# Expert stage of a hybrid decoder trunk: down weights in chunks of four row blocks by half the columns, the stationary side of the down product exchanged for the small experts, gating by two blocks, another final store

## The chip, the cores and the metric

The kernel runs on one core of a Trainium2 chip. The metric is device time in microseconds, the median of three runs. Engines are named as in the profile: PE is the matrix engine (PEld its weight loads), DVE the vector engine, ACT the scalar engine, POOL the GpSimd engine, SP the queue that issues most DMAs.

## What is computed

Two layers: a gated convolution mixer with a dense feed-forward, then an attention mixer with a routed feed-forward. The change touches only the routed one, here in the reference's words (512 tokens, `d` = 1024, hidden width 2048, 8 experts, each token goes to 2 of them):

```python
def swiglu(h, w_gate, w_up, w_down):
    return (jax.nn.silu(h @ w_gate) * (h @ w_up)) @ w_down

def moe_swiglu(h, router, w_gate, w_up, w_down):
    ...
    out = jnp.zeros_like(ht)
    for e in range(N_EXPERTS):
        out = out + gates[:, e:e + 1] * swiglu(ht, w_gate[e], w_up[e], w_down[e])
```

All of it is float32. The kernel reaches that accuracy with three products of split numbers: each float32 weight is split into a high part (`w_hi`, type fp32r) and the rest (`w_lo`, bf16); each activation likewise into `xe` (high part and rest side by side) and `xb` (bf16).

## The kernel before

**Experts and tokens.** Expert 0 comes first, then the other seven in the order of how many tokens they got. Each has room for a fixed number of tokens, its cap: 152, 152, 144, 140, 132, 128, 124, 116. An expert with a cap of at most 128 has its tokens in one part (`nh` is 1: the last three); the others have two halves (`nh` is 2). More tokens than these caps hold are left to a loop at the end (L1349 on), which does not run for these inputs.

**Chunks and steps.** An expert's weights come as 24 chunks of 1 MB, each [128 x 2048] in float32: 16 chunks for the hidden product (eight gate and eight up blocks of 128 x 128 each) and 8 for the down product (sixteen blocks: all hidden rows of one block of 128 output columns). The loop over `e` and `c` (L1275 on) is a sequence of 192 steps, one per chunk, whose code order is the order of every engine. Each step also splits one chunk ahead: ACT makes `w_hi` (L88), DVE makes `w_lo` (L97), and SP issues the load of a later chunk into a ring of raw buffers that is freed by `w_lo`.

**A hidden step** `c < 16` (`hidden_mm`, `row`): PE multiplies 16 blocks of `w_hi` (stationary) with `xe` (moving, 2 x cap columns; L1033), then 16 blocks of `w_lo` with `xb` (cap columns; L1035), into a PSUM tile `gu`. ACT and DVE add the two halves into `p2` (L1047, L1048). A step later ACT takes the SiLU into `sg` (L1053) and POOL multiplies it with the up half (L1054); another step later the result is split into `ae` and `ab` (L1058 ACT, L1059 DVE, L1060 ACT). So every one of the 16 blocks brings one SiLU, one POOL product and three split instructions.

**A down step** `c >= 16` (`down_mm`): the same 16 + 16 products, with `ae` and `ab` as moving side. Its first step keeps the last two hidden blocks for the end, since they are gated last. The result `y` has the output columns on the partitions, so it must be transposed back (`store_mm`, L1080: 4 transposes per 512 columns), scaled by the gate on ACT (`store_ev`, L1084), and added to `out` in memory row by row by an indirect, accumulating DMA that POOL issues (`store`, L1087).

**Side work of an expert.** `select` (L969, POOL): four comparisons that mark the next expert's tokens in `oh`, at steps 4 to 7. `find` (L976, PE, then small DVE operations): turns `oh` into row numbers, after step 8. `gather` (L996, POOL): an indirect DMA that fetches those rows of `hrow` into `xr`. `load_mm` and `load_ev` (L1011, L1018, L1019): transposes `xr` into the next expert's `xe`, at steps 16 to 22. The previous expert's result is transposed and stored in steps 1 to 4 with the stores issued at step 2 and, for two halves, step 13. The last expert has no next one: its transposes and its store follow its own last steps.

Of the kernel before, what the change touches and what calls it, by code (L numbers as in the profile page):

```python
# [11 lines left out]
F32 = mybir.dt.float32  # L12
# [9 lines left out]
P = 128  # L22
# [133 lines left out]
def hybrid_trunk_kernel(ctx, tc, xT_in, pos_in, vecs_in, rope_g, invf_in, ident_in, cst_in, info_in, dslot_in,  # L156
# [801 lines left out]
    class Expert:  # L958
        def __init__(s, block_row, slot, cap):
            s.block_row, s.slot, s.cap = block_row, slot, cap  # L960
            s.nh = 1 if cap <= P else 2
            s.hc = cap // s.nh
            s.p2, s.sg = {}, {}
# [59 lines left out]
        def row(s, ps, hl, n, x2, xb, flip, late=()):  # L1023

            order = [k for k in range(n) if k not in late]
            for kcs in (order, list(late)):
                for part in ((1, 0) if flip else (0, 1)):
                    for i, p in enumerate(ps):
                        for kc in kcs:
                            first = kc == order[0] and part == (1 if flip else 0)  # L1030
                            final = kc == (late or order)[-1] and part == (0 if flip else 1)
                            if part == 0:
                                mm(p[:, 0:2 * s.cap], hl[i][kc][0], x2[:, kc, :, :], start=first, stop=final)  # L1033
                            else:
                                mm(p[:, 0:s.cap], hl[i][kc][1], xb[:, kc, :], start=first, stop=final)  # L1035

        def hidden_mm(s, f, flip):
# [4 lines left out]
            b = s.block_row(2 * NB)  # L1042
            s.row([s.ps[:, 0], s.ps[:, 1]], [b[0:NB], b[NB:]], NB, s.xe, s.xb, flip)

        def hidden_add(s, f):
            p2 = s.p2[f] = ep2.tile([P, 2, CAP], F32, name="p2")[:, :, 0:s.cap]
# [9 lines left out]
        def hidden_split(s, f):  # L1056
            sg = s.sg.pop(f)
            nc.scalar.copy(s.ae[:, f, 0, :], sg)  # L1058
            tt(s.ae[:, f, 1, :], sg, s.ae[:, f, 0, :].bitcast(F32), ALU.subtract)  # L1059
            nc.scalar.copy(s.ab[:, f, :], sg)  # L1060
# [8 lines left out]
        def down_add(s, fo):  # L1069
            p2 = ep2.tile([P, 2, CAP], F32, name="p2")[:, :, 0:s.cap]  # L1070
            nc.scalar.copy(p2, s.ps[:, :, s.cap:2 * s.cap])
            tt(s.y[:, fo - 1:fo + 1, :], s.ps[:, :, 0:s.cap], p2, ALU.add)
# [19 lines left out]

    def static_row(n):
        return [ws.block() for _ in range(n)]
# [49 lines left out]
    ex = [Expert(static_row, e % 2, CAPS[e]) for e in range(NE)]  # L1144
# [128 lines left out]

    last_k = len(chunks) - 1
    for e in range(NE):  # L1275
        x, nxt, prv = ex[e], ex[e + 1] if e + 1 < NE else None, ex[e - 1] if e else None
        for c in range(24):

            out_x, g = (x, 0) if not nxt and c == NF + 5 else (prv, c - 1)
            storing = out_x and 0 <= g < 2 * out_x.nh  # L1280
            loading = nxt and NF <= c < NF + LOADS
            if storing:
                out_x.store_mm(g)
# [263 lines left out]
```

## Time and profile before

| what | value |
|---|---|
| median of three runs | 1452.95 us (1450.19 to 1458.37) |
| the profiled execution's own time | 1453.82 us |
| its span on the profile | 1452.0 us |
| PE, share of the span busy | 96% |
| DVE, ACT, POOL | 69%, 58%, 20% |
| expert stage | from about 790 us to the end |

The span is the time from the first to the last instruction of one profiled execution; the time of that execution is 1.8 us longer. Busy shares are means over very different stages. Two properties of the records must be kept in mind: the end of a matrix instruction is modelled and lies later than the start of its successor, so that the time of one is read from start to start, and short idle times between two of them disappear; and a wait for several semaphores is put down to the one that came last.

### The profile page before, as it was taken

How to read it: one execution, taken by the hardware profiler on the slowest of the kernel's cores; microseconds unless marked ns; L12 is line 12 of the kernel's file. 1: busy time of each engine (PE TensorE's matmuls, PEld its weight loads, DVE VectorE, ACT ScalarE, POOL GpSimd, SP SyncE). 2: the span in 40 equal slices, each digit the busy share in tenths (PEclk: the TensorE clock that was granted, in tenths of full speed). 3: DMA queues.
4: the chain of work that ended last, by engine and by line, in shares of the span. 5: the costliest groups of instructions: out<-in, count | busy, mean ns of one | idle time of the engine just before them, and what ended most of it. 6: DMA issues, size and time to landing. Idle time of an engine off the chain costs nothing.

```text
span 1452.0 us, 25181 instructions
## 1 busy us (share of the span) xinstructions
PE 1395.4 (96%) x10047; PEld 1230.8 (85%) x10048; DVE 1005.5 (69%) x1332; ACT 836.9 (58%) x1416; POOL 292.9 (20%) x268
## 2 busy tenths in 40 slices
PE   9999999999999999999999989999999999998994
PEld 6888888888888887878867989999999999998983
DVE  7745554432444444677778977888879898898993
ACT  6322333221222333776547768778778888888892
POOL 0000000000000000232303513416161534234240
PEclk9999999999999999999999999999999999999997
DMA  6322322232232232101126998889989999999980
GB/s 216 133 87 88 109 95 87 96 108 87 87 116 88 87 103 79 57 32 59 59 113 215 358 329 291 305 327 312 333 308 346 331 329 336 327 352 344 367 313 16
DMA packets 48884, 284.00 MB, mean 196 GB/s; under 512 B 8928, under 2 KB 10720, under 8 KB 16760
## 3 DMA queue, kind: packets, MB, share of 16 engines
q1 hardware_dynamic: 41688, 269.82, 51.7%
q0 software_dynamic: 7072, 12.51, 3.9%
q8 instruction: 81, 1.33, 0.4%
q14 instruction: 43, 0.35, 0.1%
HBM read 270.91 MB, written 11.37 MB: 194 GB/s over the span
## 4 chain that ended last, share of the span: by engine, by line
PE 70%; ACT 8%; POOL 8%; DVE 7%; issue 4%; DMA 2%; POOLq 0%; SPq 0%; ACTq 0%
PE ps L255 13%; PE ps L256 13%; PE ps L257 13%; PE gu L1033 13%; PE gu L1035 6%; ACT w_hi L88 4%; POOL sg L1054 4%; POOL oh L969 2%; DVE w_lo L97 2%; DMA xr<-hrow,ids 1%; PE ps L643 1%; POOL out L1087 1%; ACT p L1047 1%; PE ps L640 1%; ACT ae L1058 1%
## 5 line engine op out<-in xcount | busy, mean ns | idle before, releaser
L97 DVE TENSOR_TENSOR w_lo<-w_raw,w_hi 128x2048 bf16<-128x2048 f32 (+1 forms) x239 | 547.9, 2293 | 53.6 <-ACT w_hi L88 53.4
L88 ACT CAST w_hi<-w_raw 128x2048 fp32r<-128x2048 f32 x239 | 455.9, 1909 | 208.3 <-PE ps L256 157.9
L1033 PE MATMUL gu<-xe,w_hi 128*128 128x304 f32 (+6 forms) x2048 | 294.5, 297 | 0.0
L1033 PEld LDWEIGHTS gu<-xe,w_hi 128*128 128x128 f32 x2048 | 269.3, 192 | 0.1
L255 PE MATMUL ps<-xh,w_hi 128*128 128x512 f32 x592 | 232.7, 393 | 1.4 <-DVE xT L399 0.9
L256 PE MATMUL ps<-xl,w_hi 128*128 128x512 f32 x592 | 231.5, 391 | 0.0
L257 PE MATMUL ps<-xh,w_lo 128*128 128x512 f32 x592 | 231.2, 390 | 0.0
L1054 POOL TENSOR_TENSOR sg<-sg,p 128x152 f32<-128x152 f32 (+6 forms) x128 | 135.8, 1061 | 355.8 <-ACT sg L1053 352.9
L1035 PEld LDWEIGHTS <-w_lo 128*128 128x128 bf16 x3072 | 182.4, 98 | 19.7 <-DVE w_lo L97 8.2
L1033 PE MATMUL gu<-ae,w_hi 128*128 128x304 f32 (+6 forms) x1024 | 150.9, 297 | 6.0 <-DVE ae L1059 6.0
L1035 PE MATMUL gu<-xb,w_lo 128*128 128x152 bf16 (+6 forms) x2048 | 144.6, 224 | 5.2 <-DVE w_lo L97 4.3
L1033 PEld LDWEIGHTS gu<-ae,w_hi 128*128 128x128 f32 x1024 | 134.6, 190 | 8.4 <-DVE ae L1059 8.3
L255 PEld LDWEIGHTS ps<-xh,w_hi 128*128 128x128 f32 x592 | 111.6, 189 | 26.3 <-ACT xh L290 1.5
L256 PEld LDWEIGHTS ps<-xl,w_hi 128*128 128x128 f32 x592 | 111.6, 188 | 24.2 <-DVE xl L291 0.7
L257 PEld LDWEIGHTS ps<-xh,w_lo 128*128 128x128 f32 x592 | 111.6, 189 | 23.1
L248 POOL TENSOR_TENSOR rs<-m,mhalf 128x4 f32<-128x4 f32 x3 | 3.1, 1021 | 590.7 <-DVE m L505 555.8
L256 PE MATMUL ps<-al,w_hi 128*128 128x512 f32 x240 | 94.8, 395 | 0.0
L257 PE MATMUL ps<-ah,w_lo 128*128 128x512 f32 x240 | 94.8, 395 | 0.0
L255 PE MATMUL ps<-ah,w_hi 128*128 128x512 f32 x240 | 94.7, 395 | 0.0
L1048 DVE TENSOR_TENSOR p<-gu,p 128x304 f32<-128x304 f32 (+6 forms) x128 | 55.6, 434 | 27.7 <-ACT p L1047 23.3
L1035 PE MATMUL gu<-ab,w_lo 128*128 128x152 bf16 (+6 forms) x1024 | 73.6, 224 | 0.0
L1059 DVE TENSOR_TENSOR ae<-sg,ae 128x152 fp32r<-128x152 f32 (+6 forms) x128 | 51.8, 405 | 25.5 <-ACT ae L1058 25.5
(322 smaller groups left out, 1778.0 us busy)
## 6 DMA issues: line engine op xcount, KB each, us to landing
w_raw<-w_moe SPq DMA_DIRECT2D x192, 1024.0 KB, 7.3
w_raw<-w_a SPq DMA_DIRECT2D x50, 1024.0 KB, 4.9
w_raw<-w_hp SPq DMA_DIRECT2D x4, 1088.0 KB, 5.7
w_raw<-w_o SPq DMA_DIRECT2D x4, 1024.0 KB, 4.7
xT<-xT_in SPq DMA_DIRECT2D x8, 256.0 KB, 4.6
out<-hs SPq DMA_DIRECT2D x8, 256.0 KB, 3.4
hrow<-xh POOLq DMA_DIRECT2D x2, 1024.0 KB, 5.9
hrow<-xl POOLq DMA_DIRECT2D x2, 1024.0 KB, 26.3
```

Of the source, the lines that this page charges most:

```text
L88: self.nc.scalar.copy(hi[:, :w], self.raw[k][:, :w])
L97: self.nc.vector.tensor_tensor(lo[:, :w], self.raw.pop(k)[:, :w], self.hi[k][:, :w].bitcast(F32), ALU.subtract)
L255: mm(ps, wh, xh[:, kc, :], start=kc == 0, stop=False)
L256: mm(ps, wh, xl[:, kc, :], start=False, stop=False)
L257: mm(ps, wl, xh[:, kc, :], start=False, stop=kc == n - 1)
L640: mm(ps[:, 0:n], s.qT[h][a][:, q_s], s.kT[h][b][:, 0:n], start=i == 0, stop=False)
L969: nc.gpsimd.tensor_scalar(s.oh[:, tb, 0:s.cap], iota[:, 0:s.cap], p[:, tb], None, op0=ALU.is_equal)
L1033: mm(p[:, 0:2 * s.cap], hl[i][kc][0], x2[:, kc, :, :], start=first, stop=final)
L1035: mm(p[:, 0:s.cap], hl[i][kc][1], xb[:, kc, :], start=first, stop=final)
L1048: tt(p2, s.ps[:, :, 0:s.cap], p2, ALU.add)
L1054: nc.gpsimd.tensor_tensor(sg, sg, p2[:, 1], ALU.mult)
L1059: tt(s.ae[:, f, 1, :], sg, s.ae[:, f, 0, :].bitcast(F32), ALU.subtract)
```

## The change

It changes the routed experts only.

1. The host packs the down weights otherwise: a chunk is now four row blocks of 128 hidden rows by 512 of the 1024 columns, and the 8 chunks are 4 for the first half of the columns, then 4 for the second.
2. `down_mm` follows: step `k` uses the hidden blocks `4 kq` to `4 kq + 3` only (`kq = k % 4`), and its PSUM tiles live for four steps. For an expert of two halves the weights remain stationary (two PSUM tiles of two banks for half the columns). For one with at most 128 tokens `ae` and `ab` become the stationary side and the weights the moving side, 512 columns at a time, 8 + 4 products per step; the result has the tokens on the partitions, so there is no transposing back: `down_add` scales by the gate on its way out of PSUM.
3. `hidden_gate` and `hidden_split` work on two blocks at a time, every second step.
4. `select` moves to the down steps: expert `e` marks in its steps 16 to 19 for expert `e + 2` (for expert 1, expert 0 does so in its steps 2 and 3). `find` and `gather` move from step 8 to step 3 (step 6 in expert 0), and in expert 0 the ranking of the experts moves one or two steps forward.
5. A store of an expert with one part is issued in step 0 of its successor.
6. The last expert fetches its rows of `out` in step 14 (`last_base`), adds the scaled product to them on DVE and writes them back with a plain indirect DMA, one for each half of the columns, after steps 19 and 23 (`last_store`).

```diff
-        def hidden_gate(s, f):
-            sg = s.sg[f] = ep2.tile([P, CAP], F32, name="sg")[:, 0:s.cap]
-            p2 = s.p2.pop(f)
-            act(sg, p2[:, 0], AF.Silu)
-            nc.gpsimd.tensor_tensor(sg, sg, p2[:, 1], ALU.mult)
...
-        def down_mm(s, fo, flip):
-            if fo == 0:
-                s.y = late[0].tile([P, NB, CAP], F32, name="y")[:, :, 0:s.cap]
-            if fo % 2 == 0:
-                s.ps = gps.tile([P, 2, T], F32, name="gu", tag="gu")
-            s.row([s.ps[:, fo % 2]], [s.block_row(NF)], NF, s.ae, s.ab, flip, (NF - 2, NF - 1) if fo == 0 else ())
...
+            hi, lo = s.chunk()
+            for w, x, n in ((hi, s.xe, 2 * s.cap), (lo, s.xb, s.cap)):
+                for i in range(2):
+                    for kc in range(NB):
+                        b = (i * NB + kc) * P
+                        mm(s.ps[:, i, 0:n], w[:, b:b + P], x[:, kc], start=w is hi and kc == 0,
+                           stop=w is lo and kc == NB - 1)
...
+        def hidden_gate(s):
+            s.sg = ep2.tile([P, 2, CAP], F32, name="sg")[:, :, 0:s.cap]
+            act(s.sg, s.p2[:, :, 0], AF.Silu)
+            nc.gpsimd.tensor_tensor(s.sg, s.sg, s.p2[:, :, 1], ALU.mult)
+        def hidden_split(s, i):
+            f = slice(2 * i, 2 * i + 2)
+            nc.scalar.copy(s.ae[:, f, 0, :], s.sg)
+            tt(s.ae[:, f, 1, :], s.sg, s.ae[:, f, 0, :].bitcast(F32), ALU.subtract)
+            nc.scalar.copy(s.ab[:, f, :], s.sg)
+        def down_mm(s, k):
+            hi, lo = s.chunk()
+            kq = k % 4
+            if s.nh == 1:
+                if kq == 0:
+                    s.dp = gps.tile([P, 2, T], F32, name="gu", tag="gu")[0:s.cap, 0]
+                for j in range(4):
+                    for part in range(2):
+                        mm(s.dp, s.ae[:, 4 * kq + j, part, :], hi[:, j * T:(j + 1) * T],
+                           start=kq + j + part == 0, stop=False)
+                for j in range(4):
+                    mm(s.dp, s.ab[:, 4 * kq + j, :], lo[:, j * T:(j + 1) * T], start=False, stop=kq + j == 6)
+                return
+            if kq == 0:
+                s.dp = [gps.tile([P, 2, T], F32, name="gu", tag="gu") for _ in range(2)]
+            for qs in ((0, 1), (2, 3)) if kq == 3 else ((0, 1, 2, 3),):
+                for w, x, n in ((hi, s.ae, 2 * s.cap), (lo, s.ab, s.cap)):
+                    for q in qs:
+                        for j in range(4):
...
+    def last_store(q):
...
+        stt(yt, last.dp, last.gate_ap(0), last.base[:, d], op0=ALU.mult, op1=ALU.add)
+        nc.gpsimd.indirect_dma_start(
+            out=out.rearrange("t (q d) -> (t q) d", q=2),
+            out_offset=bass.IndirectOffsetOnAxis(ap=last.row2[:, q:q + 1], axis=0), in_=yt, in_offset=None)
...
-            if prv and c == 2:
+            if prv and c == (2 if prv.nh == 2 else 0):
                 prv.store(0)
...
-            if nxt and 4 <= c < 4 + TB:
-                nxt.select(posn[:, :, e + 1 - NS:e + 2 - NS], (c - 4,))
-            if nxt and c == 8:
+            if e + 2 < NE and NF <= c < NF + TB:
+                ex[e + 2].select(posn[:, :, e + 2 - NS:e + 3 - NS], (c - NF,))
+            if nxt and c == (3 if e else 6):
                 nxt.find(e + 1)
                 nxt.gather()
```

**On POOL's queue**, from the store of expert 5's result on, in expert 6 (`sg` is the product of the gating, `oh` the marks for expert 7, `xr` the gather of its rows). Before:

```order
L1087 DMA out<-yt_13398,ids_11470 664x1024
L1054 TENSOR_TENSOR sg_13541<-sg_13541,p2_13494 128x124
L1054 TENSOR_TENSOR sg_13589<-sg_13589,p2_13544 128x124
L969 TENSOR_SCALAR oh_13601<-rest_109,posn_6113 128x116
L1054 TENSOR_TENSOR sg_13639<-sg_13639,p2_13592 128x124
```

The next rows are three more pairs of `oh` and `sg`, and then the gather. Now, with the end of expert 5 ahead of it:

```order
L1047 TENSOR_TENSOR sg_12674<-sg_12674,p2_12606 128x2x128
L968 TENSOR_SCALAR oh_12685<-rest_109,posn_6113 128x116 x4
L1108 DMA out<-yt_12750,ids_10989 664x1024
L1047 TENSOR_TENSOR sg_12970<-sg_12970,p2_12886 128x2x124
L995 DMA xr_13044<-hrow_5910,ids_13036 116x1024
L1047 TENSOR_TENSOR sg_13079<-sg_13079,p2_12973 128x2x124
```

The four marks stand ahead of the store in the down steps of expert 5, the store ahead of expert 6's first gating, and one gating of two blocks between the store and the gather.

**On PE**, between steps 3 and 4 of expert 1 (`tp<-info,oh` is `find` for expert 2, `tp<-ident,y` a part of the store of expert 0's result). Before, the fourth part of the store stood alone ahead of step 4 and the 16 products of `find` four steps later; now:

```order
L975 LDWEIGHTS oh
L975 MATMUL tp<-info,oh 72x3
L1101 MATMUL tp<-ident,y 76x128 x4
L1033 MATMUL gu<-xe,w_hi 128x304 x16
L1033 LDWEIGHTS w_lo
```

The first two rows are the last of the 16 pairs of `find`. Both `find` and the store's part write a PSUM tile `tp`, of which there are two buffers.

**On ACT**, two hidden steps of expert 7. Before, each step had five instructions:

```order
L1058 CAST ae<-sg 128x116
L1060 CAST ab<-sg 128x116
L1053 ACTIVATE sg<-p_15042 128x116
L1047 COPY p_15090<-gu 128x2x116
L88 CAST w_hi<-w_raw 128x2048
```

Now two steps have seven:

```order
L1046 ACTIVATE sg<-p_14067 128x2x116
L1040 COPY p_14156<-gu 128x2x116
L88 CAST w_hi<-w_raw 128x2048
L1051 CAST ae<-sg 128x2x116
L1053 CAST ab<-sg 128x2x116
L1040 COPY p_14156<-gu 128x2x116
L88 CAST w_hi<-w_raw 128x2048
```

The gating moved ahead of the copy in every second step and the split into the other one.

## Rows read from the trace of the kernel before

**Rows 1.** The page's part 1 and 2: busy time and share of the span, and the load rate in 40 slices.

```profile
PE 1395.4 (96%) x10047; PEld 1230.8 (85%) x10048; DVE 1005.5 (69%) x1332; ACT 836.9 (58%) x1416; POOL 292.9 (20%) x268
GB/s 216 133 87 88 109 95 87 96 108 87 87 116 88 87 103 79 57 32 59 59 113 215 358 329 291 305 327 312 333 308 346 331 329 336 327 352 344 367 313 16
```

**Rows 2.** Busy time by stretch, one row for each of the experts 5 and 6 and one for the end: stretch, its length, busy time of PE, PEld, DVE, ACT and POOL with the number of instructions, granted clock of PE, DMA share, GB/s.

```profile
1206.53:1283.96 77.43, 74.49 (x805) 73.08 (x802) 68.56 (x75) 65.27 (x106) 28.24 (x23) 0.96 0.95 336
1283.96:1359.50 75.54, 70.81 (x796) 69.10 (x794) 68.62 (x75) 63.63 (x104) 29.42 (x22) 0.98 0.97 349
1429.92:1452.00 22.08, 0.82 (x8) 0.33 (x4) 0.40 (x1) 1.04 (x2) 2.11 (x1) 0.59 0.14 24
```

**Rows 3.** The waits of PE in the expert stage: who waited for whom, us in total, times, the longest.

```profile
PE tp L976 <- POOL oh L969: 10.0, 5, 3.1
PE gu L1033 <- DVE ae L1059: 6.0, 10, 0.9
PE gu L1035 <- DVE w_lo L97: 4.3, 6, 1.1
PE tp L1011 <- DMA xr<-hrow,ids: 3.8, 1, 3.8
```

**Rows 4.** PE in order of time: two undisturbed hidden steps of expert 6, then its step 9 with the wait of `find` ahead of it. Columns: start, duration, engine, line, operation, tiles, shape, count; in brackets the idle time before it and who ended it.

```profile
1321.26 2.07 PE L1033 MATMUL gu<-xe,w_hi 128*128 128x248 f32 x16
1324.02 2.08 PE L1033 MATMUL gu<-xe,w_hi 128*128 128x248 f32 x16
...
1313.85 0.43 PE L976 MATMUL tp<-info,oh 128*116 128x3 bf16 x5 [3.10 <-POOL oh L969]
1314.14 3.50 PE L1033 MATMUL gu<-xe,w_hi 128*128 128x248 f32 x16
1318.49 0.71 PE L1033 MATMUL gu<-xe,w_hi 128*128 128x248 f32 x4
```

**Rows 5.** POOL in order of time ahead of that wait, and DVE's `w_lo` at the time of the last of these rows.

```profile
1294.63 3.27 POOL L1087 DMA_INDIRECT out<-yt,ids  x1 [0.53 <-ACT yt L1084]
1297.32 2.89 POOL L1054 TENSOR_TENSOR sg<-sg,p 128x124 f32<-128x124 f32 x1
1301.08 0.45 POOL L1054 TENSOR_TENSOR sg<-sg,p 128x124 f32<-128x124 f32 x1 [0.88 <-ACT sg L1053]
1301.51 2.71 POOL L969 TENSOR_SCALAR oh<-rest,posn 128x116 bf16<-128x116 f32 x1
...
1301.56 2.28 DVE L97 TENSOR_TENSOR w_lo<-w_raw,w_hi 128x2048 bf16<-128x2048 f32 x1
```

**Rows 6.** PE in order of time: the start of the first down step of expert 6 and of the second.

```profile
1335.15 1.74 PE L1033 MATMUL gu<-ae,w_hi 128*128 128x248 f32 x13
...
1339.70 1.51 PE L1033 MATMUL gu<-ae,w_hi 128*128 128x248 f32 x11
```

**Rows 7.** DVE in order of time in a hidden step of expert 7, and PE in an undisturbed one.

```profile
1385.04 2.28 DVE L97 TENSOR_TENSOR w_lo<-w_raw,w_hi 128x2048 bf16<-128x2048 f32 x1
1387.24 0.50 DVE L1059 TENSOR_TENSOR ae<-sg,ae 128x116 fp32r<-128x116 f32 x1
1387.66 0.39 DVE L1048 TENSOR_TENSOR p<-gu,p 128x232 f32<-128x232 f32 x1
1387.97 2.28 DVE L97 TENSOR_TENSOR w_lo<-w_raw,w_hi 128x2048 bf16<-128x2048 f32 x1
...
1368.29 2.03 PE L1033 MATMUL gu<-xe,w_hi 128*128 128x232 f32 x16
1370.96 2.03 PE L1033 MATMUL gu<-xe,w_hi 128*128 128x232 f32 x16
```

**Rows 8.** PE in order of time in the dense stage: products of 512 moving columns, each with a weight load of its own.

```profile
299.90 0.39 PE L257 MATMUL ps<-xh,w_lo 128*128 128x512 f32 x1
300.13 0.39 PE L255 MATMUL ps<-xh,w_hi 128*128 128x512 f32 x1
```

**Rows 9.** All engines in order of time at the end: the first part of the last store's transposes, then the chain behind the last product.

```profile
1421.52 0.61 PE L1080 MATMUL tp<-ident,y 128*116 128x128 f32 x4
1421.88 2.03 PE L1033 MATMUL gu<-ae,w_hi 128*128 128x232 f32 x16
...
1430.12 0.35 ACT L1071 COPY p<-gu 128x232 f32<-128x232 f32 x1 [4.41 <-PE gu L1035]
1431.43 0.69 ACT L1084 ACTIVATE yt<-tp,gate 116x512 f32<-116x512 f32 x1 [0.96 <-PE tp L1080]
1432.42 2.11 POOL L1087 DMA_INDIRECT out<-yt,ids  x1 [22.64 <-ACTq L1349]
```

**Rows 10.** The page's part 6 on the four direct DMAs that write `hrow`, the first two plain, the others accumulating (KB each, us to landing); the landing time of the stores of experts 6 and 7 (the longer is expert 6's); the busy time in four microseconds while the last store runs; and the DVE instruction that is nearest to the new final addition.

```profile
hrow<-xh POOLq DMA_DIRECT2D x2, 1024.0 KB, 5.9
hrow<-xl POOLq DMA_DIRECT2D x2, 1024.0 KB, 26.3
DMA to landing us min/median/max: 13.6/18.9/24.2
1436.00:1440.00 4.00, 0.00 (x0) 0.00 (x0) 0.00 (x0) 0.00 (x0) 0.00 (x0) 0.50 0.28 48
L915 DVE SCALAR_TENSOR_TENSOR xl<-ps,r,xh x7: 737/737/740, 779.5 to 784.1; 128x512 fp32r<-128x512 f32 x7
```

**Rows 11.** ACT in order of time behind the gather of expert 1.

```profile
919.49 0.32 ACT L1058 CAST ae<-sg 128x152 fp32r<-128x152 f32 x1 [2.31 <-POOL sg L1054]
```

More of the change, by code (lines that the diff above doesn't have):

```diff
@@ L1021, in load_ev, with hidden_mm @@
                 nc.scalar.copy(s.xb, s.xe[:, :, 0, :].bitcast(F32))
[L1023 to L1037, printed above, removed]
+        def hidden_mm(s, f):
             if f == 0:
@@ new lines, in down_mm @@
+        def down_mm(s, k):
[17 more added lines that the diff above has]
+                        for j in range(4):
+                            b = j * T + q * P
+                            mm(s.dp[q // 2][:, q % 2, 0:n], w[:, b:b + P], x[:, 4 * kq + j],
+                               start=w is hi and kq + j == 0, stop=w is lo and kq + j == 6)
@@ new lines, in down_add @@
+        def down_add(s, half):
+            if half == 0:
+                if s.nh == 1:
+                    s.yt = late[0].tile([P, 2, D], F32, name="yt", bufs=1)
+                else:
+                    s.y = late[0].tile([P, NB, CAP], F32, name="y")[:, :, 0:s.cap]
+            if s.nh == 1:
+                act(s.yt[0:s.cap, 0, half * T:(half + 1) * T], s.dp, AF.Copy, scale=s.gate_ap(0))
+                return
+            for i, ps in enumerate(s.dp):
+                p2 = ep2.tile([P, 2, 2, CAP], F32, name="p2")[:, 0, :, 0:s.cap]
+                nc.scalar.copy(p2, ps[:, :, s.cap:2 * s.cap])
+                f = 4 * half + 2 * i
+                tt(s.y[:, f:f + 2, :], ps[:, :, 0:s.cap], p2, ALU.add)
@@ L1143, in hybrid_trunk_kernel @@
     nc.vector.tensor_copy(cnt, pc[:, TB, :])
-    ex = [Expert(static_row, e % 2, CAPS[e]) for e in range(NE)]
+    ex = [Expert(ws.chunk, e % 2, CAPS[e]) for e in range(NE)]
     c0 = CAPS[0]
@@ L1272, in extra_rows, with last_base @@
         nc.vector.tensor_copy(extra, nx)
+    last = ex[NE - 1]
+    assert last.nh == 1
+    def last_base():
+        last.base = late[0].tile([P, 2, D], F32, name="xr")[0:last.cap, 0]
+        nc.gpsimd.indirect_dma_start(
+            out=last.base, out_offset=None, in_=out,
+            in_offset=bass.IndirectOffsetOnAxis(ap=last.dst(0), axis=0))
+        last.row2 = fp.tile([P, 2], I32, name="row2", bufs=1)[0:last.cap]
+        at = fp.tile([P, 2], F32, name="row2f", bufs=1)[0:last.cap]
+        for q in range(2):
+            nc.vector.tensor_copy(at[:, q:q + 1], last.dst(0))
+            ts(at[:, q:q + 1], at[:, q:q + 1], 2.0, float(q), op0=ALU.mult, op1=ALU.add)
+        nc.vector.tensor_copy(last.row2, at)
+    def last_store(q):
+        d = slice(q * T, (q + 1) * T)
+        if q == 0:
+            last.yt = late[0].tile([P, 2, D], F32, name="yt", bufs=1)
+        yt = last.yt[0:last.cap, 0, d]
+        stt(yt, last.dp, last.gate_ap(0), last.base[:, d], op0=ALU.mult, op1=ALU.add)
+        nc.gpsimd.indirect_dma_start(
+            out=out.rearrange("t (q d) -> (t q) d", q=2),
+            out_offset=bass.IndirectOffsetOnAxis(ap=last.row2[:, q:q + 1], axis=0), in_=yt, in_offset=None)
     last_k = len(chunks) - 1
@@ L1309, in hybrid_trunk_kernel @@
                 prv.store(1)
+            if not nxt and c == 14:
+                last_base()
             if ws.n_split <= last_k:
@@ L1381, in hybrid_trunk_kernel @@
                                              for c in range(24)], 2, 5)
-                x = Expert(lambda n: [wx.block() for _ in range(n)], 0, CAP)
+                x = Expert(wx.chunk, 0, CAP)
                 x.src, x.dst = (lambda hf: tx[:, hf, 0:1]), (lambda hf: tx[:, hf, 1:2])
@@ L1389, in hybrid_trunk_kernel @@
                 for f in range(NF):
-                    x.hidden_mm(f, 0)
+                    x.hidden_mm(f)
                     x.hidden_add(f)
-                    x.hidden_gate(f)
-                    x.hidden_split(f)
-                for fo in range(NB):
-                    x.down_mm(fo, 0)
-                    if fo % 2:
-                        x.down_add(fo)
+                    if f % 2:
+                        x.hidden_gate()
+                        x.hidden_split(f // 2)
+                for k in range(NB):
+                    x.down_mm(k)
+                    if k % 4 == 3:
+                        x.down_add(k // 4)
                 for g in range(4):
```

74 lines of the change are left out of this document (28 added, 46 removed).

## The prediction

> **What bounds the kernel now.** The page gives PE 96% of the span [rows 1]: whatever is to be saved lies in what PE does, in what it waits for, or behind its last product. So I read the stretches of the experts next, then PE's waits, then what the waited-for engine did.
>
> The stretches [rows 2] show four things near full at once in the late experts: PE, DVE (68.6 of 77.4 us in expert 5), ACT and the DMA rings (share 0.95 to 0.97). PE's busy time hides small waits, so I take a clean step and compare: in expert 6 one hidden step lasts 1324.02 - 1321.26 = 2.76 us [rows 4], 24 of them 66 us, and the expert takes 75.5. Some 9 us there are not products of the clean kind. PE's waits [rows 3] say where: `find` waits for POOL's marks (10.0 us in five waits), the first down step for the gated blocks (6.0), `w_lo` (4.3), and in expert 0 the gathered rows (3.8). At the end 22 us pass behind the last product with PE nearly idle [rows 2].
>
> Why POOL is late with four small comparisons: its queue is in order. The store takes 3.27 us to issue and the gating behind it 2.89 [rows 5], though the same gating takes 0.45 when it meets no `w_lo`; a mark takes 2.71, and DVE runs `w_lo` for 2.28 of them. The reader should see the pattern: what POOL does beside a `w_lo` ends behind it.
>
> **The change, part by part** (all against the span of 1452.0 us; that execution's own time is 1.8 us longer, 0.9 above the median of the three runs, so the savings are taken off the median).
>
> *Marks moved to the down steps.* Between the gatings of one expert and the next POOL has nothing queued there, and `find` comes ten steps later. The 10.0 us of waiting go. With them goes what PE's clock lost behind the longest: the step behind the 3.10 us wait took 1318.49 - 1314.14 = 4.35 us instead of 2.76 [rows 4], and the granted clock of experts 5 and 6 is 0.96 and 0.98 over 77.4 and 75.5 us [rows 2], a loss of 0.04 x 77.4 + 0.02 x 75.5 = 4.6 us. **-14.6**, nothing if the wait only changes its owner (rival 2).
>
> *Down by row blocks.* The first down step needs blocks 0 to 3, gated long before; blocks 12 to 15 are due three steps later. The wait shown is 6.0 us, but the step is longer than its waits: in expert 6 it took 1339.70 - 1335.15 = 4.55 [rows 6], 1.8 above a clean one. Eight experts: 6 by the waits, 14 by this step. I take 11, nearer the step, whose start-to-start times miss nothing. **-11.**
>
> *Earlier gather in expert 0.* Two steps, some 6 us, against a wait of 3.8. **-3.8.** The ranking brought forward lengthens DVE's queue in the first steps, where DVE is the tightest engine; between nothing and the 3.8 gained: **+2**.
>
> *Gating by twos.* In expert 7 DVE needs 2.93 us a step (1385.04 to 1387.97) [rows 7], PE 2.67 (1368.29 to 1370.96) [rows 7]. DVE's share is 2.20 for `w_lo`, 0.42 for `ae`, 0.31 for `p`. One `ae` for two blocks costs between 0.42 and 0.84; I take 0.5, since `p` of 232 columns needs 0.31. Two steps: 4.40 + 0.62 + 0.5 = 5.52, or 2.76 a step: still above PE, but by 0.09 and not 0.26, over 16 steps. With the 4.3 us of waits for `w_lo` [rows 3], of which half came from queues that are now shorter: **-5** (bounds 0 and -7).
>
> *Stationary side exchanged* (24 steps). 8 + 4 products of 512 columns, each with a weight load. Rows with 512 columns start 0.23 us apart [rows 8], weight load included; 12 x 0.23 = 2.76, against 2.76 and 2.67 now [rows 4, 7] and a little more in expert 5. **0.** No row here has 512 moving bf16 columns; I take the fp32r row for it, and the 0.39 that such a row lasts is the upper bound for all twelve (rival 3). What goes are the transposes: 0.36 us for each group of four (1421.52 to 1421.88) [rows 9], two for each of experts 5 and 6 and one inside expert 7's down steps: **-1.8**. Four copies and additions per expert go from ACT and DVE, off the path. The experts of two halves switch between `w_hi` and `w_lo` twice more each: **+1**, an estimate; no row has it alone.
>
> *New waits.* (i) `find` at step 3 takes a buffer of `tp` between the third and the fourth part of the previous expert's store. The fourth part needs the buffer of the third, which ACT empties only behind step 3's copy: 0.35 + 0.69 [rows 9] and two hand-overs, some 1.2 us, of which `find` itself covers 0.5. PE waits 0.7, and behind that wait stands all of step 4. Experts 1 to 5: **+3.5** (0 to 6). (ii) The gather stands on POOL directly ahead of a gating; behind such a gather ACT waited 2.31 us for the gating [rows 11], and behind ACT's wait stand the next copy and `w_hi`. The weights are split two chunks ahead, about 5 us, so that PE feels little: 0 to 2.3 for each of five experts, I take 0.5: **+2.5**.
>
> *The end.* The last product is out at 1430.12, the store is issued at 1432.42, lands 13.6 us later and the span ends at 1452.0 [rows 9, 10]: 21.9 us. Now one DVE instruction (0.74, rows 10), 0.3 to the issue, the landing, and the same 6.0 behind it. The landing: 13.6 less 2.1 of issue is 11.5; half the bytes 5.8; a plain write of the same bytes as an accumulating one took 5.9 against 26.3 [rows 10], so half of that again at most, 2.9; with 2.1 of issue and 1 of start 6.0. Sum 13.0. **-8.9** (bounds -1.3 with the landing as now, -12 with a landing of 3). The fetched rows of `out` and the store of the first half lie beside products.
> During the last store the rings are busy to 0.28 of 16, which is 4.5 of them [rows 10]. The Trainium skill, "DMA: Bandwidth & Descriptors" (section "Why a DMA increments its semaphore by 16 and not by 1"), says that a DMA uses the largest number of engines up to 16 that divides its slowest dimension; 116 rows give 4, and the trace agrees. By that rule the plain store stays on 4 engines, as my halving assumes; were it spread over 16, the 2.9 would be 0.7 and the sum 2 us lower.
>
> **Sum:** 14.6 + 11 + 3.8 - 2 + 5 + 1.8 - 1 - 3.5 - 2.5 + 8.9 = 36.1, so 1452.95 - 36.1 = 1416.9, say **1417**. With the first down step at 14, the landing at 3, the gating at 7 and neither new wait it would be 3 + 3 + 2 + 3.5 + 2.5 = 14 lower: 1403.
>
> **Rivals.**
> 1. *DMA becomes the bound* in experts 5 to 7. Expert 6 moved 349 x 75.5 = 26.4 MB at share 0.97; at 1.00 that is 360 GB/s and 73.2 us, expert 5 (26.0 MB) 72.3, where my terms leave some 69 and 71; expert 7's 16 hidden steps at 3.0 us instead of 2.76 another 4. Together some 10: 1427. For it: the shares [rows 2]. Against: the slices reach 367 GB/s [rows 1], and several loaded chunks lie ahead when expert 5 begins.
> 2. *POOL's waiting changes its owner.* A gating of two blocks behind the gather meets a whole `w_lo`, as the 2.89 us one did [rows 5], and ACT then waits 2.3 + 2.2 at step 5, once in each of experts 1 to 6, more than the two chunks of lead allow in the shorter steps: 2.3 for each instead of 0.5, 11 more: 1428.
> The Trainium skill, "SBUF — State Buffer" (section "SBUF: two separate sides"), calls the port pair of DVE and GpSimd an exclusive lock, held for a whole instruction against a GpSimd instruction that reads SBUF; 0.45 against 2.89 us [rows 5] agrees.
> 3. *Slower:* the 512-column products with a new stationary side each time cost what one of them lasts, 0.39 us [rows 8], not the 0.23 between starts: 24 x 12 x 0.16 = 46, 1463. It decides from 0.35 us on, where 36 us are used up. Against it: the same rows, weight load included.
> 4. *The plain store is no faster:* 7.6 more, 1425.
>
> **How the numbers follow.** Forecast (1403 to 1422) 0.62; rival 1 0.14; rival 2 0.13; rival 4 0.05; rival 3 0.04; less than 7 us of gain by several of these together 0.02. The range, 1403 to 1430, holds the forecast and each of rivals 1, 2 and 4 alone. Faster by over 0.5% (7.3 us, about what a measurement of this kernel tells from no change) 0.94, within 0.02, slower 0.04.
>
> **What would show it.** Right: no wait of PE for `oh`; the first down step as long as the others; a down step of expert 7 at 2.7 to 2.8 us; granted clock 1.00 in experts 3 to 6; 13 us from the last product to the end. Wrong: PE waiting for `w_lo` in experts 5 to 7 with ACT waiting for landings (rival 1) or for `sg` (rival 2); PE waiting for `tp` by more than 1 us at step 4 would make the sum too small; so would a last landing above 8 us.

## The result and the profile after

The changed kernel takes 1411.24 us (median of four runs, 1408.37 to 1413.99) against 1453.1 us on the same chip: ratio 0.9715, 95% interval 0.9694 to 0.9736, a gain of 42 us where 36 were forecast. Run once more with the last experiments it took 1409.0 us (0.9696, 0.9673 to 0.9719).

The stretches of experts 5 and 6 and the end, to be held against [rows 2] (stretch, length, busy time of PE, PEld, DVE, ACT and POOL with instructions, granted clock, DMA share, GB/s):

```profile
1189.66:1261.07 71.41, 70.48 (x642) 62.09 (x642) 66.34 (x64) 62.00 (x80) 30.43 (x15) 1.00 1.00 356
1261.07:1330.12 69.05, 67.50 (x626) 60.64 (x625) 65.16 (x63) 60.67 (x76) 18.62 (x10) 1.00 1.01 379
...
1398.21:1412.20 13.99, 0.37 (x2) 0.00 (x0) 0.75 (x1) 0.00 (x0) 1.27 (x1) 0.62 0.08 21
```

Expert 5 is 6.0 us shorter, expert 6 is 6.5, the end 8.1; the granted clock is 1.00 instead of 0.96 and 0.98. The same reading gives 2.0, 1.5, 2.3 and 4.2 us in experts 1 to 4 and 2.3 in expert 7. Expert 0, from its own first product on, is 5.6 us shorter (878.84 - 788.74 = 90.1 before, 871.94 - 787.43 = 84.5 now). All of PE's waits in the expert stage, against [rows 3]:

```profile
PE gu L1033 <- DVE w_lo L97: 3.7, 6, 1.5
PE tp L1101 <- ACT yt L1105: 3.3, 5, 0.9
PE gu L1068 <- DVE w_lo L97: 2.3, 2, 2.0
```

The waits for marks, for the gated blocks and for the gathered rows are gone. What is left are five new waits for the `tp` buffer, and the waits for `w_lo`, 6.0 us where they were 4.3. The first down step of expert 6, against [rows 6] (PE in order of time):

```profile
1307.72 2.09 PE L1065 MATMUL gu<-w_hi,ae 128*124 128x512 f32 x8
1309.65 1.02 PE L1068 MATMUL gu<-w_lo,ab 128*124 128x512 bf16 x4
1310.51 0.26 PE L1010 MATMUL tp<-ident,xr 116*128 116x116 f32 x1
1310.54 0.70 PE L1065 MATMUL gu<-w_hi,ae 128*124 128x512 f32 x2
```

From start to start 1310.54 - 1307.72 = 2.82 us, one transpose included, where it was 4.55. Eight products with `w_hi` take 1309.65 - 1307.72 = 1.93, that is 0.24 each. The longest first down step was expert 0's, with 854.61 - 849.51 = 5.10 us before, and 847.49 - 843.97 = 3.52 now:

```profile
849.51 3.31 PE L1033 MATMUL gu<-ae,w_hi 128*128 128x304 f32 x14
854.61 2.49 PE L1033 MATMUL gu<-ae,w_hi 128*128 128x304 f32 x16
...
843.97 2.52 PE L1077 MATMUL gu<-ae,w_hi 128*128 128x304 f32 x16
847.49 2.49 PE L1077 MATMUL gu<-ae,w_hi 128*128 128x304 f32 x16
```

Read so in all eight experts, the first down step took 11.1 us more than the second in the kernel before, and takes 0.3 more now, nearly all of it in expert 7.

Where the waits for `w_lo` come from, first in expert 6 (POOL, ACT, DVE and PE in order of time, step 5 on):

```profile
1277.18 2.85 POOL L995 DMA_INDIRECT xr<-hrow,ids  x1 [6.67 <-issue]
...
1280.07 0.72 POOL L1047 TENSOR_TENSOR sg<-sg,p 128x248 f32<-128x248 f32 x1
1280.83 0.40 ACT L1051 CAST ae<-sg 128x248 fp32r<-128x248 f32 x1 [3.00 <-POOL sg L1047]
...
1281.69 1.90 ACT L88 CAST w_hi<-w_raw 128x2048 fp32r<-128x2048 f32 x1
...
1282.15 2.28 DVE L97 TENSOR_TENSOR w_lo<-w_raw,w_hi 128x2048 bf16<-128x2048 f32 x1
...
1284.49 1.04 PE L1033 MATMUL gu<-xb,w_lo 128*128 128x124 bf16 x16 [1.55 <-DVE w_lo L97]
```

Read from the last row upwards: PE waits for `w_lo`, which waited for `w_hi`, which stood behind ACT's `ae`, which waited for POOL's product, which stood behind the gather. Then in expert 7 (DVE and PE in order of time; the last row is PE's step 21):

```profile
1389.12 0.75 DVE L1313 SCALAR_TENSOR_TENSOR yt<-gu,gate,xr 116x512 f32<-116x512 f32 x1 [2.68 <-DMA xr<-out,ids]
...
1389.79 4.48 DVE L97 TENSOR_TENSOR w_lo<-w_raw,w_hi 128x2048 bf16<-128x2048 f32 x2
...
1392.12 1.02 PE L1068 MATMUL gu<-w_lo,ab 128*116 128x512 bf16 x4 [2.00 <-DVE w_lo L97]
```

The final addition waits for the fetched rows of `out`, and two `w_lo` stand behind it in DVE's queue. The end, against [rows 9]:

```profile
1397.56 1.02 PE L1068 MATMUL gu<-w_lo,ab 128*116 128x512 bf16 x4
1398.62 0.75 DVE L1313 SCALAR_TENSOR_TENSOR yt<-gu,gate,xr 116x512 f32<-116x512 f32 x1 [2.14 <-PE gu L1068]
1399.68 1.27 POOL L1314 DMA_INDIRECT out<-yt,row  x1 [6.44 <-DVE yt L1313]
```

### The profile page after: what moved, and what is told of

Same layout as the page of the kernel before. It is cut to its first block, busy times and chain, and to the rows that moved or that the text cites. A ratio compares the mean times of both kernels' runs of the same rounds, so it can differ in the third digit from the quotient of the medians.

```text
span 1412.2 us, 23783 instructions
## 1 busy us (share of the span) xinstructions
PE 1378.1 (98%) x9541; PEld 1198.7 (85%) x9544; DVE 991.5 (70%) x1263; ACT 814.8 (58%) x1210; POOL 281.2 (20%) x206
## 5 line engine op out<-in xcount | busy, mean ns | idle before, releaser
L97 DVE TENSOR_TENSOR w_lo<-w_raw,w_hi 128x2048 bf16<-128x2048 f32 (+1 forms) x239 | 555.7, 2326 | 54.2 <-ACT w_hi L88 54.2
L1033 PE MATMUL gu<-xe,w_hi 128*128 128x304 f32 (+6 forms) x2048 | 288.8, 293 | 0.0
L1033 PEld LDWEIGHTS gu<-xe,w_hi 128*128 128x128 f32 x2048 | 264.0, 189 | 0.4
L1047 POOL TENSOR_TENSOR sg<-sg,p 128x304 f32<-128x304 f32 (+6 forms) x64 | 93.8, 1465 | 310.8 <-ACT sg L1046 310.5
L1033 PEld LDWEIGHTS <-w_lo 128*128 128x128 bf16 x2048 | 120.6, 98 | 12.8 <-DVE w_lo L97 5.6
L1077 PE MATMUL gu<-ae,w_hi 128*128 128x304 f32 (+3 forms) x640 | 97.4, 302 | 0.0
L1077 PEld LDWEIGHTS gu<-ae,w_hi 128*128 128x128 f32 x640 | 87.1, 189 | 0.0
L1040 ACT COPY p<-gu 128x304 f32<-128x304 f32 (+6 forms) x128 | 49.1, 384 | 41.9 <-PE gu L1033 41.0
L968 POOL TENSOR_SCALAR oh<-rest,posn 128x152 bf16<-128x152 f32 (+6 forms) x28 | 58.0, 2084 | 1.3 <-DVE posn L1258 1.3
```

Of the source, the lines that this page charges most:

```text
L97: self.nc.vector.tensor_tensor(lo[:, :w], self.raw.pop(k)[:, :w], self.hi[k][:, :w].bitcast(F32), ALU.subtract)
L968: nc.gpsimd.tensor_scalar(s.oh[:, tb, 0:s.cap], iota[:, 0:s.cap], p[:, tb], None, op0=ALU.is_equal)
L1033: mm(s.ps[:, i, 0:n], w[:, b:b + P], x[:, kc], start=w is hi and kc == 0, stop=w is lo and kc == NB - 1)
L1047: nc.gpsimd.tensor_tensor(s.sg, s.sg, s.p2[:, :, 1], ALU.mult)
L1077: mm(s.dp[q // 2][:, q % 2, 0:n], w[:, b:b + P], x[:, 4 * kq + j], start=w is hi and kq + j == 0, stop=w is lo and kq + j == 6)
```

## The experiments

The two profiles of the changed kernel differ by 3.5 us ahead of expert 1, so beside the median stands the stretch from PE's first product of expert 1 to the end of the profiled span. For the kernel before it is 573.2 us, for the changed kernel 540.3 and 538.1 in its two profiles.

| kernel | median, us | ratio to before (95%) | from expert 1 on, us |
|---|---|---|---|
| marks undone | 1411.9 | 0.9736 (0.9699 to 0.9773) | 538.5 |
| gating undone | 1415.4 | 0.9747 (0.9716 to 0.9779) | 543.4 |
| both undone | 1427.9 | 0.9829 (0.9803 to 0.9855) | 555.0 |
| before, marks alone | 1437.2 | 0.9894 (0.9877 to 0.9910) | 562.8 |
| last blocks first | 1432.0 | 0.9868 (0.9848 to 0.9889) | 557.1 |
| exchange for expert 7 alone | 1414.8 | 0.9738 (0.9706 to 0.9770) | 543.3 |
| one accumulating store | 1415.7 | 0.9756 (0.9723 to 0.9788) | 544.6 |
| one plain store | 1412.5 | 0.9718 (0.9690 to 0.9746) | 542.4 |
| order mended, store later | 1409.6 | 0.9703 (0.9686 to 0.9721) | 537.3 |
| order mended, fetch earlier | 1403.1 | 0.9645 (0.9622 to 0.9667) | 533.4 |
| the same, cap 112 | 1399.3 | 0.9621 (0.9597 to 0.9645) | 526.5 |

**Marks undone.**

```diff
-            if e + 2 < NE and NF <= c < NF + TB:
-                ex[e + 2].select(posn[:, :, e + 2 - NS:e + 3 - NS], (c - NF,))
+            if e and nxt and 4 <= c < 4 + TB:
+                nxt.select(posn[:, :, e + 1 - NS:e + 2 - NS], (c - 4,))
...
-            if nxt and c == (3 if e else 6):
+            if nxt and c == (8 if e else 6):
```

> The changed kernel with the marks back in hidden steps 4 to 7 of the expert ahead and the search for the rows and the gather back at step 8 (from expert 1 on; expert 0 as changed). Theory (the marks wait behind POOL's queue and DVE's w_lo): PE waits for the marks again, some 10 us in five waits, plus up to 4.6 us of half clock behind the longest; the waits for the tp buffer (3.3) and those that follow the gather (some 3) go. Sum about +8: 1419 us (1414 to 1424). Rival (the marks were late because of sixteen gatings per expert, and eight of two blocks leave POOL room): no waits for marks, and without the tp waits the time falls to 1405 to 1409.

The theory fell: 1411.9 is the changed kernel's own time, and above the rival's 1405 to 1409 too. PE does wait for the marks, but by little:

```profile
PE tp L1010 <- DMA xr<-hrow,ids: 2.7, 1, 2.7
PE tp L975 <- POOL oh L968: 2.1, 3, 0.9
```

What is lost there is won by the `tp` waits that go. The rival's cause, room on POOL's queue, was put to the test next.

**Gating undone.** `hidden_gate` and `hidden_split` as in the kernel before:

```diff
-                if c > 2 and c % 2:
-                    x.hidden_split(c // 2 - 1)
-                if c and c % 2 == 0:
-                    x.hidden_gate()
+                if c > 1:
+                    x.hidden_split(c - 2)
+                if c:
+                    x.hidden_gate(c - 1)
```

> The changed kernel with the gating back to one block per step (SiLU, product and split one step apart). Theory (DVE at 2.93 us a step is what bounds expert 7, and one split per two blocks takes it to 2.76): 5 us more, 1416 us (1413 to 1419), expert 7's hidden steps at 2.93 instead of 2.67 us from the eighth on. Rival 1 (expert 7's steps were held by the landing of weights): no change, 1411. Rival 2 (a product of two blocks on POOL blocks longer, behind the gather, than one of one block): 2 to 3 us less, 1408.

4.1 us more by the medians. In expert 7 DVE stands at 2.94 us a step (1368.08 - 1365.14), where it had 2.93 before the change, and PE with it:

```profile
1365.14 2.28 DVE L97 TENSOR_TENSOR w_lo<-w_raw,w_hi 128x2048 bf16<-128x2048 f32 x1
1367.34 0.50 DVE L1051 TENSOR_TENSOR ae<-sg,ae 128x116 fp32r<-128x116 f32 x1
1367.77 0.39 DVE L1040 TENSOR_TENSOR p<-gu,p 128x232 f32<-128x232 f32 x1
1368.08 2.27 DVE L97 TENSOR_TENSOR w_lo<-w_raw,w_hi 128x2048 bf16<-128x2048 f32 x1
```

Yet expert 7 as a whole takes 67.6 us, where the two profiles of the changed kernel have 68.1 and 66.0: while its steps are slower the fetched rows of `out` land, and the wait of 2.0 us behind them is 0.7. So the time fits the theory and the place does not: what is lost lies in experts 4 to 6, which are 1.0, 0.9 and 2.2 longer, and in expert 0 with 1.4. Why there stays open.

**Both undone** (the two diffs together).

> The changed kernel with both the marks (hidden steps 4 to 7, search and gather at step 8, from expert 1 on) and the gating (one block per step) undone. Undoing the gating alone gave 1415.4, undoing the marks alone 1411.9, no more than the changed kernel. Theory (marks and gating are two cures of one wait: eight POOL products per expert instead of sixteen leave the queue free for the marks, so either alone removes it): the waits for the marks return to about 10 us with some half clock behind them, 1422 us (1419 to 1427). Rival (the marks are on time because of something else, such as the store that moved from step 2 to step 0, or the shorter down steps): 1415 us, the waits for the marks stay near 2 us.

1427.9, just above the theory's 1419 to 1427 and far from the rival's 1415. PE waits for the marks again, in experts 2 to 5:

```profile
PE tp L976 <- POOL oh L969: 7.2, 4, 2.4
```

POOL in order of time in expert 5 (steps 4 to 8) shows why, here with both undone:

```profile
1212.94 2.72 POOL L969 TENSOR_SCALAR oh<-rest,posn 128x124 bf16<-128x124 f32 x1
1215.75 0.45 POOL L1046 TENSOR_TENSOR sg<-sg,p 128x128 f32<-128x128 f32 x1
1216.19 2.71 POOL L969 TENSOR_SCALAR oh<-rest,posn 128x124 bf16<-128x124 f32 x1
...
1219.30 2.75 POOL L969 TENSOR_SCALAR oh<-rest,posn 128x124 bf16<-128x124 f32 x1
1222.02 2.50 POOL L1046 TENSOR_TENSOR sg<-sg,p 128x128 f32<-128x128 f32 x1
1224.51 0.59 POOL L969 TENSOR_SCALAR oh<-rest,posn 128x124 bf16<-128x124 f32 x1
```

The same steps of expert 5 with the marks alone undone:

```profile
1201.54 3.29 POOL L968 TENSOR_SCALAR oh<-rest,posn 128x124 bf16<-128x124 f32 x2
1206.69 0.99 POOL L1047 TENSOR_TENSOR sg<-sg,p 128x256 f32<-128x256 f32 x1 [1.87 <-ACT sg L1046]
1207.67 5.50 POOL L968 TENSOR_SCALAR oh<-rest,posn 128x124 bf16<-128x124 f32 x2
```

With one gating per step POOL has one mark and one gating to do in each step, and here, where the marks meet `w_lo`, it falls behind with no idle time in between. With one gating per two steps it is idle again behind the first pair of marks (1.87 us). So marks and gating are two cures of one wait.

They are not the only ones. In expert 6 the wait was the longest before (3.1 us, [rows 4]), and with both undone there is none. POOL there, from its first mark on:

```profile
1284.91 0.62 POOL L969 TENSOR_SCALAR oh<-rest,posn 128x116 bf16<-128x116 f32 x1
1286.83 1.08 POOL L1046 TENSOR_TENSOR sg<-sg,p 128x124 f32<-128x124 f32 x1 [1.30 <-ACT sg L1045]
1287.89 0.60 POOL L969 TENSOR_SCALAR oh<-rest,posn 128x116 bf16<-128x116 f32 x1
```

The marks begin between two `w_lo`, take 0.6 us, and POOL is idle ahead of the gating. Before, POOL's delay in this expert began with the store in step 2 and the long gating behind it [rows 5]; here that store goes out in step 0, by point 5 of the change, as the rival had it. No run has the earlier store alone, so that it is a third cure is argued and not shown.

By the medians the marks' move, its new waits included, is worth 12.5 us with gating by ones (1427.9 to 1415.4) and nothing measurable with gating by twos (1411.9 to 1411.2); gating by twos is worth 16.0 with the marks in their old place and 4.1 with them moved.

**Before, marks alone.** The kernel before with the new places of `select`, `find` and `gather` and the earlier ranking in expert 0, as in the diff of the change.

> The kernel before with only the marks moved to the down steps of the expert before, search and gather to step 3 (step 6 in expert 0, with the earlier ranking). Theory (where nothing else helps, the move is worth what the prediction gave it): no wait for marks, -10 to -14 us; the wait of 3.8 for the gathered rows in expert 0 goes; +3.5 for the tp buffer and some 3 for what follows the gather: 1441 us (1437 to 1445). Rival (POOL's waiting only changes its owner, the gathers ahead of sixteen gatings cost what the marks did): 1448 to 1453.

14.9 us less, at the theory's lower bound in time. Of these 4.3 are expert 0's (85.8 us where it was 90.1), in which search, gather and ranking moved too. No mark is waited for; the other waits of [rows 3] stand, and the new one is there:

```profile
PE gu L1033 <- DVE ae L1059: 6.8, 11, 0.9
PE gu L1035 <- DVE w_lo L97: 4.0, 5, 1.1
PE tp L1080 <- ACT yt L1084: 3.5, 5, 0.9
```

**Last blocks first.** The packing permutes the row blocks, and the last two are gated at the end of step 15:

```diff
+            fs = (0, 1, 14, 15) if kq == 0 else range(4 * kq - 2, 4 * kq + 2)
...
-                        mm(s.dp, s.ae[:, 4 * kq + j, part, :], hi[:, j * T:(j + 1) * T],
+                        mm(s.dp, s.ae[:, fs[j], part, :], hi[:, j * T:(j + 1) * T],
...
+                if c == NF - 1:
+                    x.hidden_gate()
+                    x.hidden_split(NF // 2 - 1)
```

> The changed kernel with another packing of the row blocks: the first down step takes blocks 0, 1, 14 and 15 (these two last), and the last two blocks are gated at once at the end of step 15, so that the first down step waits for the last gating again, as in the kernel before; the other chunks hold blocks 2 to 13. Theory (the choice of blocks is what removed the wait at the first down step, which took some 11 us over eight experts; here only half of a step covers the gating instead of 14 of 16 blocks, up to 1.1 us more each): 1422 to 1431 us. Rival (as with the marks, the wait is gone anyway since ACT and POOL have shorter queues): 1411 to 1415.

1432.0, 20.8 us more, just above the theory's range and far from the rival's. PE waits in the first down step of each expert:

```profile
PE gu L1066 <- ACT ae L1051: 9.1, 3, 3.4
PE gu L1081 <- DVE ae L1052: 8.6, 5, 2.2
```

So here no other part of the change hides the wait. The experiment overstates its size, above all for the last three experts, where only the `w_hi` products of two blocks cover the gating.

**Exchange for expert 7 alone.** `s.nh == 1` becomes `s.swap` in `down_mm` and `down_add`, true for the cap of 116 only; experts 5 and 6 are transposed and stored as in the kernel before.

```diff
+            s.swap = cap == CAPS[-1]
...
-            storing = prv and prv.nh == 2 and 0 < c < 5
+            storing = prv and 0 < c < 1 + 2 * prv.nh
...
-            if prv and c == (2 if prv.nh == 2 else 0):
+            if prv and c == 2:
```

> The changed kernel with the exchange kept for the last expert alone; experts 5 and 6 go back to weights as the stationary side, transposes and a store in step 2. Theory (the exchange is worth nothing in the products, only the transposes and the evacuations count): 4 x 0.36 us of transposes and two switches between w_hi and w_lo more for each of the two experts, 1413 us (1411 to 1415). Rival 1 (512 moving columns cost more than 0.23 us each): the down steps of experts 5 and 6 get shorter, 1408 or less. Rival 2 (ACT and DVE, relieved of copies and additions, were what held the late steps): 1417 or more.

3.6 us more by the medians, at the upper end of the theory's range. Its experts 5 and 6 take 72.39 and 71.23 us instead of 71.41 and 69.05, 3.2 together. Two groups of transposes of 0.36, those of expert 5's result in expert 6, are 0.7 of them (expert 6's own stand in expert 7); PE's longer wait for `w_lo` in expert 6 (2.5 us instead of 1.5) is 1.0. The other 1.5 were not traced. Rival 1 is out, since these experts get longer.

**One accumulating store, one plain store.**

```diff
-            if not nxt and c == 14:
-                last_base()
...
-                    (x.down_add if nxt else last_store)((c - NF) // 4)
+                    x.down_add((c - NF) // 4)
...
+    last.store(0)
```

> The changed kernel with the last expert stored as experts 5 and 6 are: scaled on ACT, one accumulating store of both halves behind the last product, no fetch of out. Theory (plain kind and half the bytes shorten the landing): 22 us instead of 14 from the last product to the end, less 2.4 us of DVE's wait for the fetched rows, which goes: 1417 us (1415 to 1420). Rival (the number of rows sets the landing, neither kind nor bytes): 14 to 15 us to the end, and 1409 in all.

```diff
+        if q:
+            nc.gpsimd.indirect_dma_start(
+                out=out, out_offset=bass.IndirectOffsetOnAxis(ap=last.dst(0), axis=0),
+                in_=last.yt[0:last.cap, 0, :], in_offset=None)
```

> The changed kernel with one plain store of both halves behind step 23 instead of one per half (the first half is still added up after step 19). It tells apart what shortened the landing from 13.6 us (accumulating, both halves) to 6.2 (plain, one half). Theory (both count, as the prediction had it): 9 us for the landing, some 2.5 us more than the changed kernel, 1414. Rival 1 (the kind alone): 6 to 7 us, 1411 to 1412. Rival 2 (the bytes alone): 12 to 14 us, 1417 to 1419.

The end takes 20.95 us with the accumulating store (1392.25 to 1413.20), and 17.9 with the plain one of both halves. From issue to landing the accumulating store takes 13.6 us (issued at 1393.66, landed at 1407.26), the plain one 10.3 and, in the second profile of the changed kernel, the plain one of one half 6.3: both kind and bytes count. The first run's 1415.7 lies in its theory's range; the second's 1412.5 lies between its theory and rival 1, and there the landing decides. That the accumulating store costs 4.5 us in all and not 7 is because without the fetch expert 7 is shorter, 64.5 us where the two profiles of the changed kernel have 68.1 and 66.0.

**Order mended.** The search in step 5, the gather behind the gating of step 6, in both; then the first final store in step 21, or the fetch in step 12:

```diff
-            if nxt and c == (3 if e else 6):
+            if nxt and c == (5 if e else 6):
                 nxt.find(e + 1)
+            if nxt and c == 6:
                 nxt.gather()
...
+            if not nxt and c == NF + 5:
+                last_store(0)
```

> The changed kernel with two moves: the search for the rows in step 5 and the gather behind the gating of step 6 (instead of both in step 3), and the first half's final store three quarters of the way through the last half (step 21, behind the last splits) instead of step 19. Theory (the tp wait of 3.3 us, the w_lo waits that follow the gather, some 3 us over experts 2 to 6, and the 2.4 us for which DVE's wait for the fetched rows holds w_lo in expert 7 are costs of the change that the order alone makes): 8 us less than the changed kernel, 1403 us (1401 to 1406). Rival (the weights' landing bounds experts 5 to 7, so that time won there is given back as ACT's wait for a landing): 1407 to 1411.

From expert 1 to the last product it takes 519.4 us, where the two profiles of the changed kernel have 526.3 and 524.1, but the end takes 18.0 us instead of 14.0, so that the median, 1409.6, is in the rival's range without the rival's cause. POOL in order of time there, and what it waited for:

```profile
1389.36 1.31 POOL L1316 DMA_INDIRECT out<-yt,row  x1 [14.51 <-DVE yt L1315]
...
1396.94 1.27 POOL L1316 DMA_INDIRECT out<-yt,row  x1 [6.28 <-DMA out<-yt,row]
```

The second store waits for the landing of the first and is issued 4.5 us after its data are there (DVE is done at 1392.48). So the first was put back, and the fetch moved forward instead:

```diff
-            if not nxt and c == 14:
+            if not nxt and c == 12:
                 last_base()
```

> The changed kernel with the search in step 5 and the gather behind the gating of step 6, and with the rows of out for the last expert fetched in step 12 instead of 14; the two final stores stay at steps 19 and 23. Theory (in the run with the later first store the work up to the last product took 7 us less, and only the second store, which waited 6.3 us for the landing of the first, gave 4 us back): 7 us less up to the last product and 14 us behind it, 1403.5 us (1402 to 1406). Rival (fetched earlier, those rows meet the weights' loads, land no sooner, and DVE still waits for them ahead of w_lo): 1406 to 1409.

1403.1 against 1409.0 of the changed kernel on the same chip, the theory's number. But the earlier fetch has no part in it. DVE's final addition in this run, and in the second profile of the changed kernel:

```profile
1380.74 0.75 DVE L1313 SCALAR_TENSOR_TENSOR yt<-gu,gate,xr 116x512 f32<-116x512 f32 x1 [1.71 <-DMA xr<-out,ids]
...
1383.47 0.75 DVE L1313 SCALAR_TENSOR_TENSOR yt<-gu,gate,xr 116x512 f32<-116x512 f32 x1 [1.66 <-DMA xr<-out,ids]
```

The rows take 19.8 us to land instead of 14.2, and the addition waits for them as long as it did: that is the rival's cause, though not its time. What is won is won by the order: experts 1 to 6 are 5.5 us shorter, and expert 7 takes 66.7 us, where the two profiles of the changed kernel have 68.1 and 66.0. PE waits for no `tp` buffer any more; ACT waits seven times for a landing (4.9 us), which brings up the next run.

**The same, cap 112.** `CAPS` ends in 112 instead of 116; the last expert has 106 tokens.

> As the run with the rows of out fetched in step 12, and with a cap of 112 instead of 116 for the last expert, which has 106 tokens. Theory (the number of rows decides over how many DMA engines a store spreads, 116 over 4 and 112 over 16): while the last store runs the rings are busy to well over 0.28 of 16 and for a shorter time, its landing falls from 6.2 us to 5 or less, and with 0.7 us less in the products of expert 7 the time is 1.5 to 2 us below that of the other run. Rival (the landing is latency, not engines): the same landing, 0.7 us less. The times can hardly tell these apart; the landing and the busy share in the trace do.

1399.3, the fastest kernel of this study, and 3.8 us below the other run where the theory had 1.5 to 2. Time from issue to landing of the two final stores (the shorter is the last one), in the kernel with 116 rows:

```profile
DMA to landing us min/median/max: 6.3/7.3/8.3
```

and in the one with 112:

```profile
DMA to landing us min/median/max: 3.2/6.2/9.2
```

A stretch while the last store runs (columns as above, the share of 16 DMA engines is the last but one), with 116 rows:

```profile
1393.00:1396.00 3.00, 0.00 (x0) 0.00 (x0) 0.00 (x0) 0.00 (x0) 0.00 (x0) 0.50 0.30 65
```

and with 112:

```profile
1387.00:1388.00 1.00, 0.00 (x0) 0.00 (x0) 0.00 (x0) 0.00 (x0) 0.00 (x0) 1.00 0.69 203
```

0.30 of 16 is 4.8 engines over 3 us, 0.69 is 11 over 1 us, more than four could give; the last store lands in 3.2 us instead of 6.3. The gather of expert 7's rows lands in 12.4 us instead of 24.1, the fetch of `out` in 10.2 instead of 19.8, and ACT waits for landings 2.3 us instead of 4.9. From expert 1 to the last product the kernel is 3.7 us shorter, the end 3.2; the medians show 3.8 of these 6.9. The Trainium skill, "DMA: Bandwidth & Descriptors" (section "Why a DMA increments its semaphore by 16 and not by 1"), gives 16 engines for 112 rows and 4 for 116. The shares bear it out roughly: 4.8 lies near 4, and 11 well above it.

**The changed kernel once more**, without an edit.

> The changed kernel itself once more, on the chip of these runs, so that differences of half a per cent have a base: 1411 us (1408 to 1414), 0.9715 of the kernel before. The spans that were profiled differ by up to 3 us ahead of the expert stage, and nothing behind it should.

1409.0 us, and 2 us less from expert 1 on than in its first profile; that difference is expert 7's, where the fetched rows landed in 14.2 us instead of 15.2 and PE waited 1.0 for `w_lo` where it had waited 2.3.

## Why the prediction was right, and where its steps were not

**Direction and size.** 1411 lies inside the forecast's own range. The sum held in spite of its terms: two that were added are one, some were too small, and the end was too large. By the paragraphs that follow, the end was put some 3 us too high and marks with gating, expert 0 and the exchange together some 7 too low, so that a part of the closeness is luck.

**Marks and gating by twos.** The step that failed is that -14.6 and -5 stand beside each other as if each were lost alone when its part is taken away. Moving the marks does remove the waits (1437.2 with that alone), but with gating by twos they would have all but vanished in their old place. Together the two are worth 16.6 us by the medians; the prediction's terms for them, less both new waits, give 13.6. The -5 came from DVE's step in expert 7; undone, the gating costs 4.1, but in other experts, while expert 7 gets no longer than it was in the changed kernel's first profile. Rival 2 did not come: ACT waits for the gating 15.8 us in all, but PE only a little of it.

**First down step.** -11 was right: the step's excess over the second was 11.1 us over the eight experts and is 0.3 now. Making it wait again costs 20.8 us, construction included.

**Expert 0.** 3.8 of waiting less 2 of ranking was too little; expert 0 is 5.6 us shorter. Of these 1.6 are its first down step, which belong to the -11; the 4.0 that are left are the wait of 3.8 and little else, and the earlier ranking cost nothing that shows: from the first product of expert 0 to its fourth step PE takes 10.8 us in both kernels.

**Stationary side.** 0 for the products is right, 0.24 us from start to start; -1.8 for transposes and evacuations was too small. Undoing two of three experts costs 3.2 in the trace, so that some of the switch and of DVE's and ACT's relief belongs to it; how much of each stays open.

**New waits.** The `tp` term was right to the row: 3.3 us in five waits, forecast 3.5. The one behind the gather, 2.5, has the form that was described; with both mended, experts 1 to 6 are 5.5 us shorter, 3.3 by the `tp` waits; the other 2.2 are put down to the gather.

**The end.** From the start of the final addition 13.6 us pass (1398.62 to 1412.2) against the 13.0 of the sum; the landing of 6.0 measured 6.3, and 6.1 pass behind it. But "the fetched rows of `out` lie beside products" failed: DVE's queue is in order, and its wait for them (2.68) holds two `w_lo`. So the part gives 4.5 by the run with one accumulating store, and some 5.6 with the copy and the transposes behind the last product that this run does not bring back (22.08 to 20.95), not 8.9.

**Rivals 1, 3 and 4.** In the changed kernel ACT waits once for a weight chunk (2.0 us), so DMA did not become the bound; once the order is mended it begins to show (4.9 us), and the cap of 112 halves it (2.3). Rivals 3 and 4 are refuted by 0.24 us a product and by the landings.

## What to carry to other kernels

Before two terms are added, ask whether each alone would remove the same wait; where the waits share a queue, build the four combinations, and look in each of them at every wait and not at the sum. An operation that waits for a transfer costs what stands behind it on its engine, not what stands beside it. Choose the row count of an indirect transfer with an eye to the number of engines it spreads over: four rows fewer made one land in half the time.

## What the runs showed of the hardware

In the rows above, POOL's mark takes 0.6 us, or 2.7 where it begins beside a `w_lo` of DVE, and then ends 0.4 us behind that `w_lo` [rows 5]. An indirect store of the same 116 rows lands in 13.6 us accumulating with both halves, 10.3 plain with both and 6.3 plain with one; plain with one half of 112 rows it lands in 3.2. A fetch of 116 rows issued two steps earlier took 19.8 us instead of 14.2 and came no sooner. In this program a second indirect store into `out` waits for the landing of the first: it was issued 4.5 us after its data were there.
